# One encoder layer in split float32 on one core: one PSUM tile, accumulators added two banks at a time, wider sums, other ends, and 127 instead of 126 saved-product pairs

## The chip, the cores and the metric

The kernel runs on one core of one Trainium2 chip. The metric is the device time of one execution in microseconds. The engines, with the names that the profile uses, are TensorE (PE; its weight loads are PEld), VectorE (DVE), ScalarE (ACT), GpSimd (POOL) and SyncE (SP, which here only issues transfers). TensorE writes to PSUM, which has eight banks of 512 float32 values per partition.

## The reference

One layer over 256 tokens of width 4096, all in float32. The same normalised input goes through one wide projection, whose columns feed two groups of heads; both outputs are gated and projected back, and a gated embedding is added:

```python
h = rms_norm(x, g_mix)
c_q, c_kv, k_rope, gate_a, q_b, k_b, v_b, gate_b = split(h @ w_in)      # 1024, 512, 64, 5 x 2048
q_a = rms_norm(c_q) @ w_uq ; kv = rms_norm(c_kv) @ w_ukv                # 16 heads, with rotary parts
y_a = rms_norm(softmax attention(q_a, kv)) * silu(gate_a)
y_b = rms_norm(dilated attention(q_b, k_b, v_b), three patterns) * silu(gate_b)
x = x + concat(y_a, y_b) @ w_out                                        # 4096 x 4096
x = x + (p @ w_ple) * sigmoid(rms_norm(x, g_ple) @ w_ple_gate)          # 4096 x 4096
out = rms_norm(x, g_final)
```

## The kernel before

**Products.** To reach float32 accuracy, every operand is kept as two rounded parts, hi and lo. A product of a 128x128 block with a 128x512 block is three matmuls: hi by hi, hi by lo, lo by hi (`mm`). The hi part is a copy on ScalarE, the lo part (the *remainder* below) a subtraction on VectorE (`split`). Weights come from memory in tiles of 128 rows by 1024 columns (512 KB), issued on SP's queue into four slots of `raw_all` and, in some stages, into two lent slots.

**Blocks.** A block (`Block`) is 32 such rows of weights by 1024 columns, multiplied with both halves of the tokens (t = 0, 1) into both halves of the columns (h = 0, 1). A *plain* row (letter `c`) is four products, one for each quarter. Two rows can also be taken as a *pair*: a Strassen-Winograd step that needs seven products instead of eight, at the price of sums of weight blocks (formed on VectorE in the raw slots) and of sums of activation blocks (formed once for a stage by `add_sums`). A pair is four steps, the letters `a`, `b`, `g`, `h`. Each block has an order, a string of these letters. The seven sums M1 to M7 and X take all eight banks: M2, X, M3 and M4 collect the plain rows too. M1, M5, M6 and M7 are mixed into an SBUF tile when the last pair is through (`mix`), and M2, X, M3 and M4 are added to it when the block ends, by four operations, in `d_done`, `gate_done`, `out_done` and `wide_done`. The next block starts with plain rows in the four banks just mixed; its first `a` takes a bank that one of the four adds gives back.

**Stages.** (1) The opening: x is loaded, turned by TensorE and split; small products of zeros run before it (`warm_up`). (2) Six blocks for q, k and v of the dilated heads (ORDER_D). (3) The latents, during which the dilated heads run. (4) Five blocks (ORDER_G): one for the q latent, four for the gates. (5) The latent heads. (6) The output projection (ORDER_O: three blocks, and two chunks of 512 columns without pairs); its result x1 is turned, scaled by g_ple and split, 512 columns at a time (`x1_turn`). (7) Four blocks with w_ple_gate (ORDER_P). Each ends with two rows of w_ple (letter `e`), then the sigmoid by tanh, the addition, and squares for the final norm (`wide_done`). The last one ends in `last_steps`: the rest is done token half by token half, so that the first half can be scaled and stored while the second is multiplied. `finish` forms the reciprocal root of the mean square, `scaled` multiplies and stores.

**Order of the instructions.** Instructions are not issued in the order in which the code makes them. `Metered` notes each with a duration; `Window` holds up to 200 back and lets go the one that can start first by a model of the engines (`Clock`). That the first of a bank's products come before the add which reads it, and the like, is kept by the tile framework: it finds overlapping accesses and sets the waits. Nearly all instructions bear line 293 in the profile, that of the helper which issues them; they are told apart by tiles. Banks are `m`, `s`, `o` and `t`, `lo` and `hi` are weights' parts, `B`, `Ah`, `Al`, `T` and `Q` are slots of SBUF with changing contents.

Of the kernel before, what the change touches and what calls it, by code (L numbers as in the profile page):

```python
# [19 lines left out]
P = 128  # L20
# [18 lines left out]
    "cccccccccccccccccaccccbccabcghghcccc",  # L39
    "ccccaacbbcgchgchcabgabgcahhcbaghcbghcabgacbghhcc",  # L40
    "ccabgcccabgccahbchcagbaghhacbgcbhccaghbabghghccc",
    "ccaaccbbcaghbgcghcccahcbgcaabbghgahbhghccabgchcc",
    "caaccbgabcchcgbchaagbchccbgchcgcahbgacbhaghbghcc",
    "caaccbbcggchhcabgcahbgcaahcbgbachgcbhcabgchgchcc",
# [3 lines left out]
    "ccccccacbacgbhgchabacccgbhghcaacbbgghhcccccc",  # L48
    "cccabccabghccaghbagchccbgcababahgghccbhgcabghhcc",
    "ccacbcccaabgcgchhbcgabgachchbgahbccgcaahbbgghhcc",  # L50
    "cacacbgcbcghahcbacgcbahcbgcgahcbcghahbcgabhcghcc",
)
ORDER_O = (
    "ccccacbgcccabgccacbgccahhcbhgccahabghbcghccc",
    "ccaccbcgcaahcbgcbghcabhcccgahcbaghbagcchbgchcc",
    "caccaccbbccggcabhghhcabcgchabcgacbgcchcahbghcc",
)
ORDER_P = (
    "cccaacccbgbgchhaccbagcahbgcbhgaabcgbhghhaccbghcce",
    "ccabcacbgcghccahbgchacbacgahbgaccbhcgbgahcbhghcce",  # L60
    "cabcccaccgacbghbchgacbahcgchbgabhacgbcghachbghcce",
    "ccabcacgbcghhacbgahbcghacabbcgghhccc",
# [34 lines left out]

class Clock:
# [23 lines left out]
    def ready(self, tag, bufs=1):  # L122
        old = self.tags.get(tag, ())
        return self.last(old[-bufs]) if len(old) >= bufs else 0.0

    @staticmethod
    def place(ap):
        stride = max(1, ap.ap[0][0])
        lo = ap.offset % stride
        return ap.name, lo, lo + 1 + sum((n - 1) * abs(s) for s, n in list(ap.ap)[1:])  # L130

    def after(self, ap, engine, read, alone):
        name, lo, hi = self.place(ap)
        times = [self.base.get(name, 0.0)]
        for m in self.marks.get(name, ()):
            if m[0] < hi and lo < m[1]:
                times += [t for e, t in m[2].items() if e != engine or read or e == "dve"]
                if not alone:
                    times += [t for e, t in m[3].items() if e != engine or e == "dve" and not read]
        return max(times)  # L140

    def mark(self, ap, engine, at, wrote):
        name, lo, hi = self.place(ap)
        marks = self.marks.setdefault(name, [])
        for m in marks:
            if m[0] == lo and m[1] == hi:
                break
        else:
            m = [lo, hi, {}, {}]
            marks.append(m)  # L150
        m[2 if wrote else 3][engine] = at
# [28 lines left out]
class Window:  # L180
# [10 lines left out]
    def push(self, engine, us, outs, ins, late, do, reads):  # L191
        op = Op(self.nr, engine, us, outs, ins, late, do)
        self.nr += 1
        first = set()
        line = engine if engine in self.FIFO else (engine, outs[0].name) if engine == "pe" else None
        if line and not getattr(self.tail.get(line), "gone", True):
            first.add(self.tail[line])
        self.tail[line], op.gone = op, False
        for aps, wrote in ((reads, False), (outs, True)):
            for ap in aps:  # L200
                name, lo, hi = Clock.place(ap)
                both = wrote or ap.space == bass.MemoryType.PSUM
                for other, a, b, w in self.held.get(name, ()):
                    if (both or w) and a < hi and lo < b:
                        first.add(other)
                op.spans.append((name, lo, hi, both))
# [120 lines left out]
def encoder_layer(ctx: ExitStack, tc: tile.TileContext, x, p, positions, g_mix, w_in, g_q_latent, w_uq,  # L327
# [815 lines left out]
    def gate_done(dil, c, blk):  # L1143
        def task():
            e, ps = blk.e, blk.ps
            for t, h, m in QUARTERS:
                nc.vector.tensor_tensor(e[h][:, t], e[h][:, t], ps[m], op=ALU.add)
            yield
            for h in range(2):
                for t in range(NT):  # L1150
                    nc.scalar.activation(e[h][:, t], e[h][:, t], AF.Silu, scale=rx[:, t:t + 1])
                yield
            for h in range(2):
                spawn(gate_rest(dil, c + h, e[h]))
        return task
# [55 lines left out]
    def d_done(key, blk):  # L1211
        def task():
# [3 lines left out]
            for m, t, h in quarters[2:] + quarters[:2] if key == ("v", 1) else quarters:  # L1216
                nc.vector.tensor_tensor(d[h][:, t], blk.ps[m], d[h][:, t], op=ALU.add)
# [48 lines left out]
    def x1_turn(c):  # L1266
# [4 lines left out]
        for b in range(2):  # L1271
# [7 lines left out]
            kts = slice(4 * c + 2 * b, 4 * c + 2 * b + 2)  # L1279
            split_rows(hi[:, 2 * b:2 * b + 2], lo[:, 2 * b:2 * b + 2], tp, G["ple"][:, kts])  # L1280
# [9 lines left out]
    def half_o(c):  # L1290
        def task(ps):
            yield from awaited(("res", c))
            for t in range(NT):
                nc.vector.tensor_tensor(x1[c][:, t], ps[t], x1[c][:, t], op=ALU.add)
            give(*ps.tags)
            yield
        return task

    def done_o(c):
        def task(ps):  # L1300
            for t in range(NT):
                nc.vector.tensor_tensor(x1[c][:, t], ps[t], x1[c][:, t], op=ALU.add)
# [24 lines left out]
    class Block:  # L1327
# [35 lines left out]

        def lend(self):
# [10 lines left out]
        def plain_step(self, kt):  # L1375
# [94 lines left out]
    def add_sums(n, pair, dst, tmp, name, out, free=lambda j: True, first=0):  # L1470
# [3 lines left out]
        def task():  # L1474
# [11 lines left out]
            for j0 in range(first, n, wide):  # L1486
# [3 lines left out]
                work = []  # L1490
                for j in js:
# [4 lines left out]
                for a, u, hi, lo in work:  # L1496
                    two(ALU.add, a, plain(hi), plain(lo))
                for a, u, hi, lo in work:
                    two(ALU.subtract, u[:, 0:3:2], a[:, 1:2].to_broadcast([P, 2, P]), a[:, 0:4:3])
                for a, u, hi, lo in work:  # L1500
                    two(ALU.subtract, u[:, 1], u[:, 2], a[:, 0])
                for a, u, hi, lo in work:
# [58 lines left out]
    def out_done(k, blk):  # L1561
        def task():
            quarters = ((0, 0, "M2"), (1, 1, "X"), (0, 1, "M3"), (1, 0, "M4"))
            for t, h, m in quarters:
                xc = x1[2 * k + h][:, t]
                nc.vector.tensor_tensor(xc, xc, blk.ps[m], op=ALU.add)
# [36 lines left out]
    def x1_sums():  # L1603
        return add_sums(FAST, lambda j: [q[:, 2 * (j % 2):2 * (j % 2) + 2] for q in x1T[j // 2]], z_dst, "B3",
                        "x1_sums", x1_s)
# [58 lines left out]
    def wide_done(k, blk):  # L1664
        def task():
            e, ps = blk.e, blk.ps
            quarters = ((0, 0, 0, "M2"), (3, 1, 1, "X"), (1, 0, 1, "M3"), (2, 1, 0, "M4"))
            for i, t, h, m in quarters:
                nc.vector.tensor_tensor(e[:, i], e[:, i], ps[m], op=ALU.add)
            flags.add(("added", k))  # L1670
            yield
            for n in range(6):
                for i, t, h, m in quarters[n:n + 1]:
                    nc.scalar.activation(e[:, i], e[:, i], AF.Tanh, scale=r1h[:, t:t + 1])
                for i, t, h, m in quarters[n - 1:n] if n else ():
                    u, xc = e[:, i], x1[2 * k + h][:, t]
                    nc.vector.scalar_tensor_tensor(u, u, 1.0, P4[t, h], op0=ALU.add, op1=ALU.mult)
                    nc.vector.tensor_tensor(xc, u, xc, op=ALU.add)
                for i, t, h, m in quarters[n - 2:n - 1] if n > 1 else ():
                    nc.scalar.activation(e[:, i], x1[2 * k + h][:, t], AF.Square, accum_out=ss2[:, t, 2 * k + h:2 * k + h + 1])  # L1680
                if n == 4:
                    flags.add(("wide", k))
                yield
# [230 lines left out]
    x_s, x_s2, z = {}, {}, {}  # L1914

    def xz_dst(j):
        if j > 3:
            return slot(("T0", "T1", "T2", "T3", "T4", "T7")[j - 4], [2, 4, P], F32R)
# [5 lines left out]
    def x_sums():  # L1924
        return add_sums(max(FAST_QKV), x_pair, xz_dst, "B1", "x_sums", x_s,
                        lambda j: ("x", j if j < 4 else 7) in flags and (j < 9 or "rotary" in flags))
# [18 lines left out]
    for n, key in enumerate((key, i) for i in range(2) for key in "qkv"):  # L1945
# [3 lines left out]
                    ("D", (("T5", 1), ("T6", 1)), n == 5), WP + ["B4", "B6", "B0", "B1"] + [("T4", "T7")] * (max(FAST_QKV) < 9))  # L1949
# [4 lines left out]
        if n == 0:  # L1954
            opening = blk
            for x_ in steps[:16]:
                x_.ring = WP
        for at, tag in ((2, "B0"), (3, "B6"), (4, "B4"), (5, "B1")):
            allow(blk, tag, lambda i, at=at, n=n, tag=tag, end=mid_step: (n < at or n == at and i < end) and (
                tag != "B1" or ("x_sums", max(FAST_QKV) - 1) in flags))  # L1960
# [332 lines left out]
```

## Time and profile before

| | |
|---|---|
| three runs | 1886.6, 1886.74 (median), 1888.31 us |
| profiled execution | 1886.92 us |
| its span | 1885.2 us |
| granted clock | 0.998 |
| matmuls | 9103 |
| pairs, by stage | 42 (D), 34 (G), 20 (O), 30 (P): 126 |

The span runs from the first to the last instruction on the core; the execution's own time is 1.7 us longer. Rows of the profile read: engine, line, operation, what is written `<-` what is read, size of a tile as partitions x elements. In the views by time the first two numbers are the start and the length in us. A value in brackets is idle time of the engine before the row and what ended it. In the table by stretches the columns are the stretch, its length, the busy times of PE, PEld, DVE, ACT and POOL with the count of instructions, the granted clock, the DMA share, and GB/s.

### The profile page before, as it was taken

What the parts mean: (1) busy time and instruction counts of PE and PEld (TensorE: products, weight loads), DVE (VectorE), ACT (ScalarE), POOL (GpSimd) and SP (SyncE); (2) the same over time, 40 slices, a digit from 0 to 9 for tenths busy, and PEclk for the clock granted to TensorE, in tenths of its full rate; (3) what the DMA queues carried; (4) which work ended last, traced back from release to release, by engine and by line L of the source; (5) the groups of instructions that cost most, each with busy time, mean ns of one, the idle gap of its engine ahead of it and who ended that gap; (6) DMA issues with size and microseconds to landing.
All of it is one profiled execution on the core that took longest, in us unless ns stands there. A gap on an engine that the chain in (4) does not pass through costs nothing.

```text
span 1885.2 us, 25442 instructions
## 1 busy us (share of the span) xinstructions
PE 1868.0 (99%) x9103; PEld 1575.8 (84%) x9103; DVE 1720.6 (91%) x2333; ACT 1178.7 (63%) x1590; POOL 28.6 (2%) x41
## 2 busy tenths in 40 slices
PE   9999999999999999999999999999999999999996
PEld 7888888888899888888888999888888888888885
DVE  6999999899989989999999777899899989999997
ACT  7666565556688565656566656655556656666664
POOL 0000000000001000000000000000000000000000
PEclk9999999999999999999999999999999999999999
DMA  8666666566735556565667554666666566566674
GB/s 284 217 201 206 217 193 212 190 219 194 216 93 152 177 191 216 182 213 187 213 204 202 137 144 126 197 213 201 213 206 218 181 217 221 190 213 201 200 233 170
DMA packets 160871, 370.58 MB, mean 197 GB/s; under 512 B 29116, under 2 KB 70952, under 8 KB 160744
## 3 DMA queue, kind: packets, MB, share of 16 engines
q1 hardware_dynamic: 159896, 366.58, 61.2%
q0 software_dynamic: 512, 1.84, 0.3%
q8 instruction: 71, 1.16, 0.3%
q10 hardware_dynamic: 336, 0.54, 0.1%
q14 instruction: 56, 0.46, 0.1%
HBM read 364.72 MB, written 4.19 MB: 196 GB/s over the span
## 4 chain that ended last, share of the span: by engine, by line
PE 94%; DVE 3%; DMA 1%; ACT 1%; issue 0%; DVEq 0%; ACTq 0%
PE m L293 54%; PE t L293 19%; PE s L293 12%; PE o L293 10%; DVE lo L293 1%; DMA raw_all<-in_w_ple_dram 1%; DVE T L293 0%; DVE Ah L293 0%; ACT hi L293 0%; DMA raw_all<-in_w_ple_gate_dram 0%; DVE B L293 0%; DMA Al<-in_w_out_dram 0%; DVE Al L293 0%; DVE st L293 0%; DVE raw_all L293 0%
## 5 line engine op out<-in xcount | busy, mean ns | idle before, releaser
L293 ACT ACTIVATE hi<-raw_all 128x1024 fp32r<-128x1024 f32 (+2 forms) x417 | 409.8, 989 | 251.4 <-PE m L293 77.5
L293 DVE TENSOR_TENSOR lo<-raw_all,hi 128x1024 fp32r<-128x1024 f32 (+2 forms) x417 | 468.6, 1133 | 52.7 <-ACT hi L293 49.8
L293 PE MATMUL m<-hi,Ah 128*128 128x512 f32 (+2 forms) x666 | 247.3, 387 | 0.5 <-ACT hi L293 0.5
L293 PE MATMUL m<-hi,Al 128*128 128x512 f32 (+2 forms) x622 | 228.4, 380 | 0.0
L293 PE MATMUL m<-lo,Ah 128*128 128x512 f32 (+2 forms) x543 | 205.4, 378 | 0.9 <-DVE lo L293 0.8
L293 ACT ACTIVATE B<-raw_all 128x1024 fp32r<-128x1024 f32 (+2 forms) x144 | 140.3, 978 | 80.7 <-DVE raw_all L293 23.7
L293 DVE TENSOR_TENSOR raw_all<-raw_all 128x512 f32<-128x512 f32 (+1 forms) x239 | 172.2, 722 | 3.8 <-DMA raw_all<-in_w_out_dram 0.5
L293 DVE TENSOR_TENSOR B<-raw_all,B 128x1024 fp32r<-128x1024 f32 (+2 forms) x144 | 160.8, 1120 | 14.8 <-ACT B L293 14.4
L293 PE MATMUL m<-hi,B 128*128 128x512 f32 (+1 forms) x476 | 164.4, 390 | 0.0
L293 PE MATMUL m<-B,Ah 128*128 128x512 f32 (+2 forms) x560 | 149.1, 359 | 0.0
L293 PEld LDWEIGHTS m<-hi,Ah 128*128 128x128 f32 x666 | 125.3, 188 | 23.4 <-ACT hi L293 1.3
L293 PEld LDWEIGHTS m<-hi,Al 128*128 128x128 f32 x622 | 116.9, 188 | 21.8
L293 PEld LDWEIGHTS m<-lo,Ah 128*128 128x128 f32 x543 | 102.3, 188 | 18.8 <-DVE lo L293 1.6
L293 PEld LDWEIGHTS m<-B,Ah 128*128 128x128 f32 x560 | 97.2, 189 | 14.4
L293 PEld LDWEIGHTS m<-hi,B 128*128 128x128 f32 x476 | 89.2, 188 | 17.7
L293 PE MATMUL m<-B,Al 128*128 128x512 f32 (+2 forms) x286 | 99.2, 371 | 0.0
L293 ACT ACTIVATE hi<-B 128x1024 fp32r<-128x1024 f32 (+1 forms) x65 | 64.6, 999 | 46.3 <-PE m L293 14.0
L293 PE MATMUL m<-lo,B 128*128 128x512 f32 (+1 forms) x238 | 92.2, 387 | 0.0
L293 PE MATMUL t<-hi,Ah 128*128 128x512 f32 x216 | 81.6, 391 | 0.0
L293 DVE TENSOR_TENSOR lo<-B,hi 128x1024 fp32r<-128x1024 f32 (+1 forms) x65 | 74.3, 1145 | 4.7 <-ACT hi L293 3.9
L293 ACT ACTIVATE hi<-T 128x1024 fp32r<-128x1024 f32 (+1 forms) x43 | 44.4, 1038 | 35.1 <-DVE T L293 13.5
L293 PE MATMUL t<-lo,Ah 128*128 128x512 f32 x165 | 64.3, 389 | 0.0
(486 smaller groups left out, 4286.5 us busy)
## 6 DMA issues: line engine op xcount, KB each, us to landing
raw_all<-in_w_in_dram SPq DMA_DIRECT2D x254, 512.0 KB, 4.4
raw_all<-in_w_out_dram SPq DMA_DIRECT2D x98, 512.0 KB, 4.7
raw_all<-in_w_ple_gate_dram SPq DMA_DIRECT2D x90, 512.0 KB, 5.0
T<-in_w_in_dram SPq DMA_DIRECT2D x58, 512.0 KB, 4.5
B<-in_w_in_dram SPq DMA_DIRECT2D x47, 512.0 KB, 4.6
Ah<-in_w_ple_gate_dram SPq DMA_DIRECT2D x38, 512.0 KB, 4.8
raw_all<-in_w_uq_dram SPq DMA_DIRECT2D x48, 256.0 KB, 3.6
B<-in_w_out_dram SPq DMA_DIRECT2D x18, 512.0 KB, 4.8
```

Of the source, the lines that this page charges most:

```text
L293: self.window.push(key, us, outs, ins, late, lambda: do(out, *rest, **named), reads)
```

## The change

1. *PSUM is one tile.* `bank` cuts a bank out of one tile of eight; the order of the banks in it is new, and the planner (`Clock.places`) treats each bank of it by itself. Two banks at any distance can be read by one operation (`banks`, `Block.two`).
2. *Finished accumulators are added two banks at a time*: M2 with M4, then M3 with X, in all four closing functions, and both token halves of a 512-column chunk of the output projection together.
3. *Sums for two pairs at once* in `add_sums`, where a stage asks for it (`x_sums`, `x1_sums`).
4. *x1 remainders:* ScalarE scales the turned columns in place in PSUM, and hi and lo are then formed by one plain copy and one plain subtraction of 512.
5. *`wide_done`* applies tanh to a whole token half at once and joins two of the products with the embedding.
6. *The opening:* the first half of the first two rows of weights is split before the x columns, and the second row is loaded in two halves as the first was.
7. *The end:* for the second token half, `finish` uses Sqrt, a reciprocal and one refinement, instead of an integer estimate and three refinements.
8. *Orders:* most strings are new; the last gate block has nine pairs instead of eight: 127. It also needs a ninth set of sums.

```diff
 ORDER_G = (
...
-    "cacacbgcbcghahcbacgcbahcbgcgahcbcghahcbgcabhcghcc",
+    "cacabaghcbgcbcghhacbagchabcgbhgacbcghhcababgcghhcc",
...
 ORDER_P = (
...
-    "ccabcacgbcghhacbgahbcghacabbcgghhccc",
+    "cccabcgchaabgchbcgahbcghaabcgbghhccc",
...
+BANKS = "m0", "m2", "s", "t0", "m1", "m3", "o", "t1"
...
-    def bank(tag, shape, bufs=1):
-        names[tag] = names.get(tag, 0) + 1
-        return made(lambda: pp.tile([P, *shape], F32, tag=tag, name=f"{tag}_{names[tag]}", bufs=bufs), tag, bufs)
+    psum = pp.tile([P, len(BANKS), 512], F32, tag="psum", name="psum")
+
+    def bank(tag, shape):
+        v = psum[:, BANKS.index(tag), :math.prod(shape)]
...
+    def banks(*tags):
+        a, b = (BANKS.index(t) for t in tags)
+        return psum[:, a:b + 1:b - a]
...
-            for t, h, m in QUARTERS:
-                nc.vector.tensor_tensor(e[h][:, t], e[h][:, t], ps[m], op=ALU.add)
+            for h in range(2):
+                nc.vector.tensor_tensor(e[h], e[h], blk.two(h), op=ALU.add)
...
-            split_rows(hi[:, 2 * b:2 * b + 2], lo[:, 2 * b:2 * b + 2], tp, G["ple"][:, kts])
+            for k in range(2):
+                nc.scalar.activation(tp[:, k], tp[:, k], AF.Copy, scale=G["ple"][:, 4 * c + 2 * b + k:4 * c + 2 * b + k + 1])
+            split(hi[:, 2 * b:2 * b + 2], lo[:, 2 * b:2 * b + 2], tp)
...
+        def two(self, h):
+            return banks(*(self.tags[m] for m in (("M2", "M4"), ("M3", "X"))[h]))
...
-            for lo, n in ((0, Q), (Q, Q)) if self.late and kt == 16 else ((0, 2 * self.q),):
+            for lo, n in ((0, Q), (Q, Q)) if self.late and kt in (16, 17) else ((0, 2 * self.q),):
...
                 if kt in self.front:
-                    self.front.pop(kt)()
                     for h in range(2):
                         split(hi[:, h], lo[:, h], box[0][:, h])
+                        if h == 0:
+                            self.front.pop(kt)()
...
+                if twice:
+                    a, u = both[:, :, :4], both[:, :, 4:]
+                    hi, lo = (q.rearrange("p (j k) (t c) -> p j (k t) c", j=2, t=NT) for q in both_at(j0))
+                    two(ALU.add, a, plain(hi), plain(lo))
+                    two(ALU.subtract, u[:, :, 0:3:2], a[:, :, 1:2].to_broadcast([P, 2, 2, P]), a[:, :, 0:4:3])
...
+            nc.scalar.activation(e[:, 2:], e[:, 2:], AF.Tanh, scale=r1h[:, 1:])
+            yield
+            nc.scalar.activation(e[:, :2], e[:, :2], AF.Tanh, scale=r1h[:, :1])
+            nc.vector.scalar_tensor_tensor(e[:, 2:], e[:, 2:], 1.0, banks("t0", "t1"), op0=ALU.add, op1=ALU.mult)
...
     def finish(t, a):
         r, h, w = r2[:, t:t + 1], stat(1), stat(1)
-        bits = r.bitcast(I32)
-        nc.vector.tensor_scalar(bits, a.bitcast(I32), -0.5, float(0x5F3759DF), op0=ALU.mult, op1=ALU.add)
         nc.vector.tensor_scalar(h, a, -0.5, None, op0=ALU.mult)
-        for _ in range(3):
+        if t:
+            nc.scalar.activation(w, a, AF.Sqrt)
+            nc.vector.reciprocal(r, w)
+        else:
+            nc.vector.tensor_scalar(r.bitcast(I32), a.bitcast(I32), -0.5, float(0x5F3759DF), op0=ALU.mult, op1=ALU.add)
+        for _ in range(1 if t else 3):
             nc.vector.scalar_tensor_tensor(w, r, r, h, op0=ALU.mult, op1=ALU.mult)
             nc.vector.scalar_tensor_tensor(r, w, 1.5, r, op0=ALU.add, op1=ALU.mult)
```

More of the change, by code (lines that the diff above doesn't have):

```diff
@@ L126, in place, with places @@
     @staticmethod
[L127 to L130, printed above, removed]
-    def after(self, ap, engine, read, alone):
[L133 to L139, printed above, removed]
+    def places(ap):
+        dims = list(ap.ap)
+        lo, name = ap.offset % max(1, dims[0][0]), ap.name
+        if name[:4] != "psum":
+            return [(name, lo, lo + 1 + sum((n - 1) * abs(s) for s, n in dims[1:]))]
+        n, dims = (dims[1], dims[2:]) if len(dims) > 2 and dims[1][0] >= 512 else ((0, 1), dims[1:])
+        width = 1 + sum((n - 1) * abs(s) for s, n in dims)
+        starts = [lo + k * n[0] for k in range(n[1])]
+        return [(f"psum{a // 512}", a % 512, a % 512 + width) for a in starts]
@@ L140, in after @@
+    def after(self, ap, engine, read, alone):
+        times = [0.0]
+        for name, lo, hi in self.places(ap):
+            times.append(self.base.get(name, 0.0))
+            for m in self.marks.get(name, ()):
+                if m[0] < hi and lo < m[1]:
+                    times += [t for e, t in m[2].items() if e != engine or read or e == "dve"]
+                    if not alone:
+                        times += [t for e, t in m[3].items() if e != engine or e == "dve" and not read]
         return max(times)
@@ L142, in mark @@
     def mark(self, ap, engine, at, wrote):
[L143 to L151, printed above, removed]
+        for name, lo, hi in self.places(ap):
+            marks = self.marks.setdefault(name, [])
+            if wrote and name[:4] == "psum":
+                marks[:] = [m for m in marks if m[0] < lo or hi < m[1]]
+            for m in marks:
+                if m[0] == lo and m[1] == hi:
+                    break
+            else:
+                m = [lo, hi, {}, {}]
+                marks.append(m)
+            m[2 if wrote else 3][engine] = at
@@ L200, in push @@
             for ap in aps:
-                name, lo, hi = Clock.place(ap)
                 both = wrote or ap.space == bass.MemoryType.PSUM
[L203 to L206, printed above, removed]
+                for name, lo, hi in Clock.places(ap):
+                    for other, a, b, w in self.held.get(name, ()):
+                        if (both or w) and a < hi and lo < b:
+                            first.add(other)
+                    op.spans.append((name, lo, hi, both))
         for name, *span in op.spans:
@@ L1215, in task @@
             quarters = ("M2", 0, 0), ("X", 1, 1), ("M3", 0, 1), ("M4", 1, 0)
[L1216 to L1217 removed]
+            for h in range(2):
+                nc.vector.tensor_tensor(d[h], blk.two(h), d[h], op=ALU.add)
             yield from awaited("rx")
@@ L1292, in task @@
             yield from awaited(("res", c))
-            for t in range(NT):
-                nc.vector.tensor_tensor(x1[c][:, t], ps[t], x1[c][:, t], op=ALU.add)
+            nc.vector.tensor_tensor(x1[c], banks(*ps.tags), x1[c], op=ALU.add)
             give(*ps.tags)
@@ L1300, in task @@
         def task(ps):
-            for t in range(NT):
-                nc.vector.tensor_tensor(x1[c][:, t], ps[t], x1[c][:, t], op=ALU.add)
+            nc.vector.tensor_tensor(x1[c], banks(*ps.tags), x1[c], op=ALU.add)
             give(*ps.tags)
@@ L1563, in task @@
             quarters = ((0, 0, "M2"), (1, 1, "X"), (0, 1, "M3"), (1, 0, "M4"))
-            for t, h, m in quarters:
-                xc = x1[2 * k + h][:, t]
-                nc.vector.tensor_tensor(xc, xc, blk.ps[m], op=ALU.add)
+            for h in range(2):
+                xc = x1[2 * k + h]
+                nc.vector.tensor_tensor(xc, xc, blk.two(h), op=ALU.add)
             yield
```

113 lines of the change are left out of this document (68 added, 45 removed).

## The prediction

> **What bounds the kernel now.** I read the page first, then the table by stretches, the waits of TensorE, the chain of waits, and last the instructions in order of time at both ends and at one boundary of two blocks.
>
> ```profile
> span 1885.2 us, 25442 instructions
> PE 1868.0 (99%) x9103; PEld 1575.8 (84%) x9103; DVE 1720.6 (91%) x2333; ACT 1178.7 (63%) x1590; POOL 28.6 (2%) x41
> PE m L293 <- DVE junk L293: 1.5, 1, 1.5
> PE m L293 <- DVE lo L293: 1.0, 2, 0.8
> PE m L293 <- ACT hi L293: 0.5, 1, 0.5
> PE s L293 <- ACT T L293: 0.4, 1, 0.4
> 236.93 6.12 PE m L293 x27
> ```
>
> The first two rows are the page's; the next four are all that TensorE waited for (total, times, longest); the last is a stretch of the chain. TensorE is busy 99% of the span, and its waits that have a name come to 3.4 us. In the chain 27 products of 512 columns take 6.12 us, 0.227 each. So time comes off in three ways only: fewer matmuls, fewer of those few waits, and a shorter head and tail where TensorE does not yet, or no longer, run. Shorter work on VectorE or ScalarE is worth nothing by itself.
>
> The profiled execution took 1886.92 us, 1.7 more than its span. That is 0.18 above the median of the runs (1886.74), so I add the terms to 1886.92 and take 0.2 off at the end.
>
> **The extra pair.** The orders hold 126 pairs before (42+34+20+30) and 127 after; the new one is the ninth of the last gate block. Two plain rows of weights cost eight products, a pair seven; each product is three matmuls. Three matmuls of 0.227 are **0.68 us less**, the only matmuls that go. The price is on VectorE:
>
> ```profile
> 936.45 0.68 DVE L293 TENSOR_TENSOR B7b<-B7b,o 128x512 f32<-128x512 f32 x1
> 937.05 0.68 DVE L293 TENSOR_TENSOR B7b<-B7b,t 128x512 f32<-128x512 f32 x1
> 938.85 1.22 DVE L293 TENSOR_TENSOR lo<-raw_all,hi 128x1024 fp32r<-128x1024 f32 x1
> 939.98 1.22 DVE L293 TENSOR_TENSOR B<-raw_all,B 128x1024 fp32r<-128x1024 f32 x1
> 1572.00:1654.00 82.00, 82.00 (x364) 67.89 (x363) 79.69 (x94) 52.16 (x64) 0.00 (x0) 1.00 0.62 207
> 934.00:1016.00 82.00, 82.00 (x364) 67.89 (x363) 76.54 (x89) 49.38 (x53) 0.00 (x0) 1.00 0.66 194
> ```
>
> Starts of adjoining operations lie 0.60 apart for 512 elements and 1.13 for 1024. A pair has one remainder of 512, three of 1024 and four sums of 512: 0.60 + 3.39 + 2.40 = 6.4. Two plain rows have two remainders, 2.26. So VectorE gets about 4.1 us more in this block. The last row is that block: VectorE (the third busy time) works 76.5 of 82 us and rests 5.5. After: 5.5 - 4.1 - 0.7 of shorter block + 0.1 saved by the merged adds leaves 0.8. The row above it is a block of the last stage, where 2.3 us of rest were enough for TensorE to lose nothing; 0.8 is beyond anything this trace shows. I put 0.2 us of new waiting there; between 0 and the 1.5 that are missing against 2.3. The ninth pair's own sums (four operations of up to 512 and one remainder, about 3 us) fall to earlier blocks with 5 us of rest.
>
> **Merged adds, one PSUM tile.** A block ends with four adds of an accumulator; now two adds take two banks each. From the rows above that is 1.13 instead of 1.20 us, 0.07 each, some 38 times: 2.7 us of VectorE under a running TensorE, worth nothing. What it adds is a wait. The first add takes M2 and M4, and M4 is the block's last product:
>
> ```profile
> 934.31 0.39 PE L293 MATMUL t<-hi,Al 128*128 128x512 f32 x1
> 935.25 0.68 DVE L293 TENSOR_TENSOR B7a<-B7a,s 128x512 f32<-128x512 f32 x1
> 937.25 0.62 PE L293 MATMUL s<-B,Ah 128*128 128x512 f32 x2
> ```
>
> Here the block before ends at 934.70, the add of M2 (bank s) starts 0.55 later anyway, and bank s is written again at 937.25, when the next block opens its first pair. With two banks the add ends near 936.5 and still leaves 0.7. Behind a waiting add on VectorE stand the remainders of the next block's first rows, and TensorE waits for those. I take 0; the bounds are 0 and the third rival's price.
>
> **Two-pair sums, x1 remainders.**
>
> ```profile
> L293 ACT ACTIVATE T<-t 128x512 fp32r<-128x512 f32 x56 | 33.3, 595 | 12.4 <-PE t L293 11.9
> L293 DVE SCALAR_TENSOR_TENSOR Al<-t,gT,Ah 128x256 fp32r<-128x256 f32 x30 | 13.1, 476 | 1.0 <-ACT Ah L293 0.9
> ```
>
> The remainder of two x1 columns is now one plain subtraction of 512 instead of two scaled ones of 256 at 0.48, so VectorE saves 0.2; ScalarE scales in place and then copies, 0.6 more (first row). Sixteen times that is 3 us less on VectorE and 10 us more on ScalarE, which rests 37% of the span. Each chunk is ready some 0.4 us later; the rows of weights that need it come microseconds later. The wide closing of the last stage and the sums of two pairs cut VectorE's fixed part by under 0.1 per operation. Together 0; if ScalarE had no rest where they fall, each of the 16 would cost up to 0.6, and nothing in the trace points to that.
>
> **The head.**
>
> ```profile
> 5.28 1.31 PE L293 MATMUL m<-junk 128*128 128x512 bf16 x3
> 6.21 0.62 PE L293 MATMUL m<-hi,Ah 128*128 128x512 f32 x1
> 6.93 0.50 PE L293 MATMUL m<-lo,Ah 128*128 128x512 f32 x1
> 7.28 0.40 PE L293 MATMUL m<-hi,Al 128*128 128x512 f32 x1
> 4.48 0.20 ACT L293 ACTIVATE gT<-t 128x32 f32<-128x32 f32 x1 [1.97 <-PE t L293]
> 5.16 0.47 ACT L293 ACTIVATE Ah<-s,gT 128x256 fp32r<-128x256 f32 x1 [0.49 <-PE s L293]
> 6.19 1.29 DVE L293 TENSOR_TENSOR lo<-raw_all,hi 128x512 fp32r<-128x512 f32 x2
> ```
>
> From the first to the third product pass 1.07 us where two steps of 0.227 would be 0.46: 0.61 is lost, because the weights' first remainder runs at 6.19, behind the scaled copy of x. After, the first half of the weights goes ahead: its copy fits into ScalarE's pause after 4.68, its remainder starts near 5.4 and is done by 6.1. The three warm-up products still hold TensorE until 6.2, so nothing before that is won. **0.5 us**, between 0 and 0.6. The second row of weights also comes in halves: one more issue on SP's queue, ahead of loads that are needed later.
>
> **The tail.**
>
> ```profile
> 1872.31 0.49 ACT L293 ACTIVATE Ah<-Ah,st 128x256 f32<-128x256 f32 x1
> 1876.05 1.33 ACT L293 ACTIVATE T<-T,st 128x512 f32<-128x512 f32 x2 [3.25 <-DVE st L293]
> 1874.21 0.46 DVE L293 TENSOR_SCALAR st<-st 128x1 f32<-128x1 f32 x3
> 1874.71 1.31 DVE L293 SCALAR_TENSOR_TENSOR st<-st 128x1 f32<-128x1 f32 x6
> 1057.96 0.17 DVE L293 RECIPROCAL st<-st 128x2 f32<-128x2 f32 x1 [2.60 <-ACT T L293]
> ```
>
> The reciprocal root of the last 128 tokens takes from 1874.21 to 1876.05, and all that is left to scale and store waits for it. After: the mean (0.25), a Sqrt on ScalarE (0.20, as the small copy at 4.48), a reciprocal (0.20), one refinement instead of three (a third of 1.35, 0.45), two hand-overs of some 0.05: 1.2 instead of 1.85. **0.65 us less**, at most 0.75, if the function table of Sqrt is loaded in ScalarE's 3.25 us of rest. Loads of tables in this trace:
>
> ```profile
> 98.21 1.28 ACT L293 ACT_TABLE_LOAD   x1
> 99.77 0.26 ACT L293 ACTIVATE ss<-T 128x64 f32<-128x64 f32 x1 [0.28 <-DVE T L293]
> 1055.43 1.28 ACT L293 ACT_TABLE_LOAD   x1 [2.13 <-DVE st L293]
> 1056.73 0.56 ACT L293 ACTIVATE T<-s,st 128x256 f32<-128x256 f32 x1
> ```
>
> At 98.21 the load ran at once, and only the activation behind it waited for VectorE. At 1055.43 the load itself stood 2.13 us behind VectorE. There the activation reads PSUM too; the new Sqrt reads one value of VectorE alone, like the first, so I take the first: loaded from 1872.8 to 1874.1, before 1874.46. [...]
>
> **The new orders, above all in the last block.**
>
> ```profile
> 1848.17 0.86 PE L293 MATMUL s<-Ah,B 128*128 128x512 f32 x3
> 1849.54 0.49 PE L293 MATMUL m<-hi,Ah 128*128 128x512 f32 x1 [0.50 <-ACT hi L293]
> 1850.79 0.50 PE L293 MATMUL m<-lo,Ah 128*128 128x512 f32 x1 [0.77 <-DVE lo L293]
> 1824.64 0.39 PE L293 MATMUL m<-hi,Al 128*128 128x512 f32 x1
> 1825.25 0.50 PE L293 MATMUL m<-lo,Al 128*128 128x512 f32 x1 [0.22 <-DVE lo L293]
> 1841.25 7.07 DMA raw_all<-in_w_ple_dram
> ```
>
> Against steps of 0.227, TensorE loses 0.69 before 1849.54, 1.02 before 1850.79 and 0.38 before 1825.25, with some 0.2 of restart: 2.3 us. The last row (the chain) shows why: a load of w_ple issued at 1841.25 landed 7.07 us later. The loads are issued when VectorE has read a slot, so a late VectorE makes late loads. The new order begins this block with three plain rows instead of two, keeps the two lent slots two steps longer, and the merged work spares VectorE 0.2 us. I take **1.0 us less**. The bounds are all 2.3 back and as much again.
>
> **The sum.** -0.68 + 0.2 - 0.5 - 0.65 - 1.0 = -2.6; 1886.92 - 2.6 = 1884.3, against the median 1884.1.
>
> **Rivals.** (1) The orders remove the last block's waits wholly: -0.68 - 0.6 - 0.75 - 2.3 = -4.3, 1882.4. For it: the waits are few and at one place. Against: they come from a queue of loads whose number does not change. (2) Sqrt's table load stands behind VectorE's signal as at 1055.43: 1.28 more, 1885.4. Against: the row at 98.21. [...] (3) The slow one: a merged add gives the bank back too late. Five blocks open their pair after one plain row (2.72 us). The row at 935.25 left 0.7 of slack; with one remainder (1.13) more before the add TensorE waits 0.4, with two 1.5. Five times 1.5 is 7.7: 1891.8. It decides from two on; one gives 1886.2. Against: the planner that orders the instructions knows this bank, and the slack shown. (4) The waits treat the one PSUM tile as a span, so that TensorE stands from 934.53 until both adds are over, near 937.6: 3.1 us at 17 block ends, 53 us, 1937. Nothing before shows such a view. (5) The last block gets as much worse: 1884.1 + 1.0 + 2.3 = 1887.4, with the new saturated gate block on top at most 1888.7.
>
> **How the numbers follow.** Forecast 0.38, rivals 0.25, 0.17, 0.07, 0.03 and 0.10. A measurement of this kernel tells about 0.2% from no change, 3.8 us: faster lies below 1883.0, slower above 1890.5. Faster holds most of (1), 0.21, and the low edge of the forecast, 0.07: 0.28. Slower holds (3) and (4): 0.10. The rest, 0.62, is no change. The range 1881.7 to 1887.6 takes in (1), (2) and most of (5).
>
> **What would show it.** 9100 products on TensorE instead of 9103; the third product 0.46 us after the first; the load of Sqrt's table right behind the last tanh and the root 1.2 us after its mean; VectorE over 97% in the last gate block, with TensorE's waits there; TensorE's waits after 1820. I am wrong if TensorE waits at block ends for an accumulator's add, or if all named waits exceed 5 us.

## The result, and the profile after

| | before | after |
|---|---|---|
| median of the runs | 1887.45 us (4 runs) | 1937.17 us (4 runs, 1934.37 to 1939.61) |
| ratio | | 1.0263, 95% interval 1.0247 to 1.0273 |
| profiled span | 1885.2 us | 1937.8 us |
| matmuls | 9103 | 9100 |
| VectorE operations | 2333 | 2259 |

The kernel became 2.6% slower. The forecast was 1884.1 us; the number that came true is the fourth rival's, 1937, to which I had given a chance of 0.03. That its sum fits so closely is partly luck, as the waits below show.

The page of the kernel after, its span and the busy times:

```profile
span 1937.8 us, 25374 instructions
PE 1884.3 (97%) x9100; PEld 1577.0 (81%) x9100; DVE 1727.9 (89%) x2259; ACT 1194.0 (62%) x1604; POOL 30.2 (2%) x41
```

VectorE has 74 operations fewer, yet its busy time did not fall: a wide operation costs nearly what its two halves cost (1.13 us against 1.20 in the prediction's rows), and the ninth pair's sums came on top. TensorE's share fell from 99% to 97%: it stands still now. What it waits for is told by the waits of TensorE after (total, times, longest):

```profile
PE psum L306 <- DVE B L306: 21.7, 20, 2.9
PE psum L306 <- DVE T L306: 8.8, 9, 1.4
PE psum L306 <- DVE B7a L306: 3.6, 3, 1.3
PE psum L306 <- DVE B7b L306: 2.9, 3, 1.3
PE psum L306 <- DVE junk L306: 1.5, 1, 1.5
```

The first four rows, which the kernel before did not have, come to 37.0 us; all its named waits were 3.4 us. `B`, `T`, `B7a` and `B7b` are the tiles to which finished accumulators are added. They are 35 waits of at most 2.9 us, about 1 us each, and not 17 of 3.1 as the fourth rival has it: its place and its sum came true, its price only at the first block end. The rest of the 50 us goes with the restart behind each wait (after the one at 188.28 the next product starts 0.34 us later instead of 0.227) and with stretches at half the clock (0.50 near 106 us, 0.51 near 191, 0.57 near 794); how it divides was not measured. The instructions in order of time, TensorE and VectorE, where the first block ends:

```profile
101.95 0.39 PE L306 MATMUL psum<-B,Al 128*128 128x512 f32 x1
102.74 2.35 DVE L306 TENSOR_TENSOR B<-psum,B 128x1024 f32<-128x1024 f32 x2
105.24 0.76 PE L306 MATMUL psum<-hi,Ah 128*128 128x512 f32 x1 [2.90 <-DVE B L306]
105.80 0.63 PE L306 MATMUL psum<-lo,Ah 128*128 128x512 f32 x1
...
107.93 0.57 PE L306 MATMUL psum<-hi,Ah 128*128 128x512 f32 x1
108.34 0.40 PE L306 MATMUL psum<-lo,Ah 128*128 128x512 f32 x1
```

The block's last product starts at 101.95. The next block's weights are ready, and its first product goes to a bank that neither merged add reads, yet it starts at 105.24, behind both adds (102.74 to 105.09). From start to start that is 3.29 instead of 0.227: 3.06 us lost; the prediction's price for rival 4 was 3.1. The products behind it are 0.43 apart instead of 0.227, up to 108.34. The table by stretches says why; the eighth column is the granted clock:

```profile
102.00:105.00 3.00, 0.34 (x2) 0.00 (x0) 3.00 (x3) 1.69 (x3) 0.00 (x0) 0.98 0.83 253
106.50:108.00 1.50, 1.50 (x5) 1.11 (x5) 1.50 (x3) 1.50 (x3) 0.00 (x0) 0.50 0.09 38
108.00:110.00 2.00, 2.00 (x10) 1.62 (x9) 2.00 (x4) 0.82 (x2) 0.00 (x0) 0.93 0.75 193
190.00:197.00 7.00, 5.95 (x14) 4.70 (x15) 5.69 (x6) 1.91 (x3) 0.00 (x0) 0.51 0.53 174
```

Behind the stall TensorE is granted half the clock (0.50), and once more after the second block's end (0.51).

Both ends did what was predicted. The instructions after, the opening and then the last reciprocal root:

```profile
6.05 0.58 PE L306 MATMUL psum<-hi,Ah 128*128 128x512 f32 x1
6.46 0.39 PE L306 MATMUL psum<-lo,Ah 128*128 128x512 f32 x1
6.69 0.40 PE L306 MATMUL psum<-hi,Al 128*128 128x512 f32 x1
...
1925.67 0.49 ACT L306 ACTIVATE Ah<-Ah,st 128x256 f32<-128x256 f32 x1
1926.18 1.28 ACT L306 ACT_TABLE_LOAD   x1
1927.58 0.40 DVE L306 TENSOR_SCALAR st<-st 128x1 f32<-128x1 f32 x2
1927.82 0.20 ACT L306 ACTIVATE st<-st 128x1 f32<-128x1 f32 x1 [0.36 <-DVE st L306]
1928.70 1.33 ACT L306 ACTIVATE T<-T,st 128x512 f32<-128x512 f32 x2 [0.68 <-DVE st L306]
```

The third product starts 0.64 after the first (1.07 before, 0.46 at best) and the first 0.16 earlier: 0.59 gained. From the start of the mean to the scaling pass 1.12 us instead of 1.84. From the last matmul to the end of the span it is 12.83 us instead of 13.58.

### The profile page after: what moved, and what is told of

It is laid out like the page before. It is cut to its first block, busy times and chain, and to the rows that moved or that the text cites. A ratio compares the mean times of both kernels' runs of the same rounds, so it can differ in the third digit from the quotient of the medians.

```text
span 1937.8 us, 25374 instructions
## 1 busy us (share of the span) xinstructions
PE 1884.3 (97%) x9100; PEld 1577.0 (81%) x9100; DVE 1727.9 (89%) x2259; ACT 1194.0 (62%) x1604; POOL 30.2 (2%) x41
## 3 DMA queue, kind: packets, MB, share of 16 engines
q0 software_dynamic: 512, 1.84, 0.3%
## 4 chain that ended last, share of the span: by engine, by line
PE 85%; DVE 10%; issue 2%; ACT 1%; DMA 1%; DVEq 0%; ACTq 0%; SPq 0%
PE psum L306 85%; DVE B L306 3%; DVE lo L306 2%; DVE T L306 2%; DVE raw_all L306 1%; ACT hi L306 1%; DMA raw_all<-in_w_in_dram 0%; DVE Ah L306 0%; DVE B7b L306 0%; DVE Al L306 0%; DMA raw_all<-in_w_ple_dram 0%; ACT T L306 0%; DVE st L306 0%; DMA raw_all<-in_w_out_dram 0%; ACT B L306 0%
## 5 line engine op out<-in xcount | busy, mean ns | idle before, releaser
L306 PE MATMUL psum<-hi,Ah 128*128 128x512 f32 (+2 forms) x1089 | 403.9, 392 | 18.4 <-DVE B L306 9.5
L306 PE MATMUL psum<-hi,Al 128*128 128x512 f32 (+2 forms) x965 | 355.3, 385 | 2.6 <-DVE B7a L306 1.3
L306 PE MATMUL psum<-lo,Ah 128*128 128x512 f32 (+2 forms) x875 | 337.4, 386 | 6.1 <-DVE B L306 2.6
L306 PEld LDWEIGHTS psum<-hi,Ah 128*128 128x128 f32 x1089 | 205.7, 189 | 65.7 <-DVE T L306 9.8
L306 PE MATMUL psum<-hi,B 128*128 128x512 f32 (+1 forms) x754 | 254.4, 390 | 1.3 <-DVE B L306 0.7
L306 PE MATMUL psum<-B,Ah 128*128 128x512 f32 (+2 forms) x847 | 237.9, 370 | 2.3 <-DVE B7b L306 1.3
L306 PEld LDWEIGHTS psum<-hi,Al 128*128 128x128 f32 x965 | 182.6, 189 | 39.2 <-DVE B7a L306 1.7
L306 PEld LDWEIGHTS psum<-lo,Ah 128*128 128x128 f32 x875 | 165.9, 190 | 38.4 <-DVE B L306 3.4
L306 PEld LDWEIGHTS psum<-B,Ah 128*128 128x128 f32 x847 | 151.1, 189 | 28.6 <-DVE B7b L306 1.8
L306 PE MATMUL psum<-B,Al 128*128 128x512 f32 (+2 forms) x482 | 167.0, 379 | 2.6 <-DVE B7a L306 1.3
```

The costliest lines, as they stand in the source:

```text
L306: self.window.push(key, us, outs, ins, late, lambda: do(out, *rest, **named), reads)
```

## The experiments

Two questions were open: which part of the change makes TensorE stand, and whether the rest brings the 2.6 us that I forecast. Each run's time stands beside a median of the kernel before on the same chip (1886.91 to 1887.73).

**1. Without the two-bank operations.** The other closing functions and the second tanh gate go back in the same way.

```diff
-            for h in range(2):
-                nc.vector.tensor_tensor(e[h], e[h], blk.two(h), op=ALU.add)
+            for t, h, m in QUARTERS:
+                nc.vector.tensor_tensor(e[h][:, t], e[h][:, t], ps[m], op=ALU.add)
...
```

> The changed kernel with every two-bank operation on VectorE undone: the accumulators are added one bank at a time again, in the order of before, and the second tanh gate is multiplied bank by bank; the one PSUM tile, the new orders, both ends and the x1 sums stay. Theory W (an operation over two banks of the one tile is held apart from products into every bank of that tile): without such operations there is nothing to be held apart; TensorE's waits on VectorE's adds at block ends go from about 37 us back to a few, and the time is my forecast, about 1884.5 us (1882 to 1888). Theory S (held apart only from products into banks between its two) and theory A (the two-bank operation itself gives its banks back too late) say the same here. Theory O (one tile for all banks costs by itself, also for single-bank operations) says about 1937 us. Theory N (the loss comes from the new orders, the head or the tail) says about 1937 us too.

Measured 1893.32 us, ratio 1.0033 (1.0022 to 1.0045). 44 of the 50 us are the two-bank operations. One tile for all of PSUM is not what costs (theory O falls). But 1893 is not 1884.5: some 6 us more than before come from elsewhere, against 2.6 less that I had forecast.

**2. Neighbouring banks.** The banks get new numbers, and X and M4 change their places; two lines left out here let the planner cut a contiguous access into its banks. Every operation stays.

```diff
-BANKS = "m0", "m2", "s", "t0", "m1", "m3", "o", "t1"
+BANKS = "m0", "m1", "m2", "m3", "s", "o", "t0", "t1"
...
-        NAMES = "M2", "X", "M3", "M4", "M1", "M5", "M6", "M7"
+        NAMES = "M2", "M4", "M3", "X", "M1", "M5", "M6", "M7"
```

> The changed kernel with the banks numbered so that the two banks of every merged operation are neighbours: no bank lies between them any more; one PSUM tile and the merged operations stay. Theory S: no product is held up by a merged operation on other banks, about 1884.5 us (1882 to 1888), TensorE's named waits on VectorE's adds a few us. Theory W: every merged operation still holds up the products into the six other banks: about 1937 us (1925 to 1945), 25 to 40 us of named waits. Theories A, O and N: about 1937 us.

Measured 1894.24 us, ratio 1.0033 (1.002 to 1.0047): the same as without the operations. The same block end in this kernel, in order of time:

```profile
102.68 0.39 PE L308 MATMUL psum<-hi,Ah 128*128 128x512 f32 x1
102.85 2.35 DVE L308 TENSOR_TENSOR B<-psum,B 128x1024 f32<-128x1024 f32 x2
102.91 0.39 PE L308 MATMUL psum<-lo,Ah 128*128 128x512 f32 x1
...
105.17 0.39 PE L308 MATMUL psum<-hi,Al 128*128 128x512 f32 x1
```

The adds take the same 2.35 us, and TensorE multiplies under them without a gap. W falls, and S holds: a merged add holds up products into its two banks and *all banks between them*. After the change M2 and M4 of the first block are banks 0 and 5 of the tile, M3 and X banks 1 and 4, and the next block's plain rows go to 2, 6, 3 and 7. So half of the banks that TensorE wants next lie inside; at the end of the second block it is 4 and 5 between 2 and 7.

One more reading would fit these times: that an add of two banks apart counts as one of all eight. The kernel after decides against it. At the end of its fourth block the adds take banks 2 and 7, and 3 and 6; the next block opens with bank 0, outside both, and goes on with bank 4, inside both:

```profile
356.70 1.22 DVE L306 TENSOR_TENSOR B<-psum,B 128x1024 f32<-128x1024 f32 x1
356.98 0.39 PE L306 MATMUL psum<-hi,Ah 128*128 128x512 f32 x1
357.21 0.39 PE L306 MATMUL psum<-lo,Ah 128*128 128x512 f32 x1
357.44 0.39 PE L306 MATMUL psum<-hi,Al 128*128 128x512 f32 x1
357.97 0.50 PE L306 MATMUL psum<-hi,Ah 128*128 128x512 f32 x1
```

The three matmuls for bank 0 run under the first of the adds (356.70 to 357.92); the first one for bank 4 starts when it is over.

**3. Four tiles of two banks.**

```diff
-    psum = pp.tile([P, len(BANKS), 512], F32, tag="psum", name="psum")
+    psum = [pp.tile([P, 2, 512], F32, tag="psum" + q, name="psum" + q) for q in "ABCD"]
```

> The same as the kernel with neighbouring banks, but PSUM is four tiles of two banks instead of one tile of eight, so that a merged operation's tile holds only the two banks that it adds. Theories W and S: a merged operation holds up only products into its own two banks; about 1884.5 us (1881 to 1888), named waits on VectorE's adds a few us. Theory A (the merged operation itself is what costs, since a bank comes free 0.5 us later): about 1937 us. Theory O: between the two at most. Theory N: about 1937 us.

> The kernel with four PSUM tiles of two banks, without any two-bank operation. Theory T (in a tile that is smaller than all of PSUM, a read of one bank holds up products into the tile's other bank): the waits in the heads' stages stay, about 1940 to 1945. Theory M (the merged operations cost there after all): about 1893.

Measured 1944.69 us, ratio 1.0302 (1.0284 to 1.0319), and without any two-bank operation 1951.58 us, ratio 1.034 (1.0326 to 1.0354). W and S missed by 60 us. A and N come near the size, but the waits are not where they put them: most lie in the heads' stages, and taking out the merged operations, in the second run, makes nothing faster. T, which was formed on the first trace, holds. The instructions of the first of these kernels in the latent heads' stage, and then the two largest waits of TensorE in the second:

```profile
1071.52 0.40 PE L310 MATMUL psumA<-B,hi 128*128 128x256 f32 x2
1072.02 0.69 DVE L310 TENSOR_TENSOR B<-psumA,B 128x512 fp32r<-128x512 f32 x1 [1.11 <-PE psumA L310]
1072.77 0.38 PE L310 MATMUL psumA<-B,lo 128*128 128x256 f32 x1 [0.85 <-DVE B L310]
```

```profile
PE psumC L310 <- DVE T L310: 4.9, 6, 1.0
PE psumD L310 <- DVE T L310: 4.2, 8, 0.9
```

The matmul at 1072.77 is the third of a product whose first two have run, and it waits for VectorE's reading of the same tile. The program reads a bank only when its product is finished, so VectorE reads the other one. An operation that reads *one* bank of a two-bank tile holds up the products into the tile's other bank, here by 0.85 us. In the heads' stages, where the two banks of a tile serve different units, this happens over and over. So the tile of all eight banks tells its banks apart when an operation stays in one of them (1893.32 us without two-bank operations), while the smaller tiles do not (1951.58 us, also without).

**4. The merges alone, apart and neighbouring.** To the kernel before are added only the one tile and the two-bank adds; the second run numbers the banks as in experiment 2. Orders, wide steps, x1 remainders and both ends stay as before.

```diff
+    psum = pp.tile([P, len(BANKS), 512], F32, tag="psum", name="psum")
...
-            for t, h, m in QUARTERS:
-                nc.vector.tensor_tensor(e[h][:, t], e[h][:, t], ps[m], op=ALU.add)
+            for h in range(2):
+                nc.vector.tensor_tensor(e[h], e[h], blk.two(h), op=ALU.add)
...
```

> The kernel of before with one part of the change alone: PSUM as one tile and the accumulators of closed blocks and units added two banks at a time (38 two-bank operations); the orders of before with 126 pairs, the wide steps of before behind the adds, and both ends of before. Theories W, S and A: the whole loss is in this part, about 1935 us (1925 to 1945) against 1887.5, with 25 to 40 us of TensorE's named waits on VectorE's adds and stretches of products at half the granted clock behind the longest of them. Theory O: about the same. Theory N: about 1887.5 us (1886 to 1890), no new waits.

> The kernel of before with one PSUM tile and the two-bank adds, as in the run of the merges alone, but with the banks numbered so that the two of each merged add are neighbours. Theory S (a merged add holds up products into all banks between its two): the 50 us of the run of the merges alone vanish; 1887.5 to 1889, TensorE's named waits 3 to 6 us. If the neighbours are not what counts: 1935 or more.

Measured 1938.74 us, ratio 1.0279 (1.0261 to 1.0296), against 1889.59, ratio 1.0011 (1.0002 to 1.0019). The merges with banks apart cost 51 us against the median beside them, and the numbering of the banks alone is worth 49 of these. And the merged adds are not free even side by side: 2 to 3 us. Two waits of TensorE that the kernel before does not have show where some of it is lost, in the output projection; in the second, TensorE turns x1 and waits until the add of both token halves is through:

```profile
1495.18 0.50 PE L308 MATMUL psum<-lo,B 128*128 128x512 f32 x1 [0.66 <-DVE lo L308]
...
1524.81 0.65 PE L308 MATMUL psum<-ident,T 128*128 128x128 f32 x4 [0.60 <-DVE T L308]
```

**5. The x1 remainders.** Undone in the kernel of experiment 2, and made alone in the kernel before.

```diff
-            for k in range(2):
-                nc.scalar.activation(tp[:, k], tp[:, k], AF.Copy, scale=G["ple"][:, 4 * c + 2 * b + k:4 * c + 2 * b + k + 1])
-            split(hi[:, 2 * b:2 * b + 2], lo[:, 2 * b:2 * b + 2], tp)
+            kts = slice(4 * c + 2 * b, 4 * c + 2 * b + 2)
+            split_rows(hi[:, 2 * b:2 * b + 2], lo[:, 2 * b:2 * b + 2], tp, G["ple"][:, kts])
```

> The kernel with neighbouring banks, with the x1 remainders of before (scaled copy and scaled subtraction of 256 columns each, nothing scaled in place). Theory X (the bank in which x1 is turned comes back later by the in-place scaling, and TensorE's next product wants that bank): the two waits of TensorE at 1322 and 1414 us of that kernel (2.2 and 2.6 us, and half-clock products behind the second) go; some 5.5 to 6.5 us less, 1887 to 1888. Theory R (the new orders of the output projection put the product behind the turn, whatever the remainder costs): the waits stay, 1893.

> The kernel of before with the x1 remainders of the change alone. Theory X: waits of TensorE for a turned bank appear in the output projection here too, some 2 to 6 us more, 1890 to 1893. Theory R: no such waits, 1887.3. My prediction's step: 0.

Measured 1890.96 us, ratio 1.0016 (1.0007 to 1.0025), and 1890.13, ratio 1.0012 (1.0003 to 1.002). Undoing gains 3 us, making it alone costs 2 to 3: theory X. It is not the whole of it, though: X put the first run at 1887 to 1888, and of the two waits named, the one at 1322 went, the one at 1414 stayed. The kernel of experiment 2 at that place, in order of time:

```profile
1413.98 0.40 PE L308 MATMUL psum<-hi,B 128*128 128x512 f32 x1
1414.24 0.91 ACT L308 ACTIVATE psum<-psum,gT 128x256 f32<-128x256 f32 x2
1415.18 0.60 ACT L308 ACTIVATE B<-psum 128x512 fp32r<-128x512 f32 x1
1416.21 0.69 DVE L308 TENSOR_TENSOR B<-psum,B 128x512 fp32r<-128x512 f32 x1
1416.95 0.80 PE L308 MATMUL psum<-hi,B 128*128 128x512 f32 x1 [2.57 <-DVE B L308]
```

x1 is turned in a bank that a block uses too. TensorE's next product goes into this bank and waits for the scaling (0.91), the copy (0.60), a stretch in which VectorE finishes another remainder, and the subtraction (0.69). With the old remainders it waits just as long, since VectorE is behind by three other operations:

```profile
1412.91 0.87 DVE L308 SCALAR_TENSOR_TENSOR B<-psum,gT,B 128x256 fp32r<-128x256 f32 x2
1413.84 0.50 PE L308 MATMUL psum<-hi,B 128*128 128x512 f32 x1 [2.71 <-DVE B L308]
```

Alone in the kernel before, the change of the remainders makes a new wait at another turn (1320 us). In the waits of TensorE it is the row

```profile
PE o L293 <- DVE Al L293: 1.7, 1, 1.7
```

**6. The orders of the output projection.** The kernel of experiment 5's first run, with the three strings of ORDER_O of before.

```diff
-    "ccccacbccabgcgccacbgccahhbhgcccabghhabcghccc",
-    "ccacbccgcahcbaghcbgcabhcacgcbghchabagcchbgchcc",
-    "caccaccbbcggccabhghhcabcgcabcchgabgcahchbgchcc",
+    "ccccacbgcccabgccacbgccahhcbhgccahabghbcghccc",
+    "ccaccbcgcaahcbgcbghcabhcccgahcbaghbagcchbgchcc",
+    "caccaccbbccggcabhghhcabcgchabcgacbgcchcahbghcc",
```

> The kernel with neighbouring banks and the x1 remainders of before, with the three orders of the output projection of before as well. Theory R for the wait at 1411 us (2.7 us, which stayed when the x1 remainders were undone): the new orders put a product into the bank of the turn right behind it; it goes, and 1890.96 becomes 1887 (1886 to 1888). Otherwise it stays and the time is 1891.

Measured 1888.09 us, ratio 1.0006 (0.9997 to 1.0015), just above the range expected. The wait of 2.71 is gone; the span falls from 1889.4 to 1886.2, with one wait of 0.8 more at 1494. So this wait, which began at 1411, belonged to the new orders.

**7. The parts with a gain, alone.** The kernel before with the last stage's orders and both ends of the change; the first run also has the ninth pair (the first string below) and its ninth set of sums. `finish` and the opening are as the change has them.

```diff
-    "cacacbgcbcghahcbacgcbahcbgcgahcbcghahbcgabhcghcc",
+    "cacabaghcbgcbcghhacbagchabcgbhgacbcghhcababgcghhcc",
...
-    "cccaacccbgbgchhaccbagcahbgcbhgaabcgbhghhaccbghcce",
-    "ccabcacbgcghccahbgchacbacgahbgaccbhcgbgahcbhghcce",
-    "cabcccaccgacbghbchgacbahcgchbgabhacgbcghachbghcce",
-    "ccabcacgbcghhacbgahbcghacabbcgghhccc",
+    "cccaccacbgbgchahcbcagbcahgcbhgabcgabhchgcahbgchce",
+    "ccabcacbcgcghchabcgachbacgahbgaccbhgcbgahcbhghcce",
+    "cabcaccccgbgachhbcgacbhacbgagcbhghahcbcgahcbghcce",
+    "cccabcgchaabgchbcgahbcghaabcgbghhccc",
...
+            nc.scalar.activation(w, a, AF.Sqrt)
+            nc.vector.reciprocal(r, w)
```

> The kernel of before with only those parts of the change that I gave a gain: the ninth pair of the last gate block, the orders of the four blocks with w_ple_gate, the split of the first weights ahead of x, and the end with Sqrt; PSUM, adds, sums and x1 remainders of before. My prediction's terms: -0.68 (pair), +0.2 (VectorE's last gate block), -0.5 (head), -0.65 (tail), -1.0 (waits of the last block): 1887.3 - 2.6 = 1884.7, between 1883 and 1886. If the terms don't add up or the orders need the merged adds: 1887 or more.

> The kernel with the gaining parts alone, without the ninth pair and its ninth set of sums (126 pairs, all orders but the last stage's as before). Theory P (the ninth pair costs more on VectorE than its three matmuls save: a wait of 1.2 us at 786 us, where the ninth sums are formed, and 0.5 in the last gate block): no wait at 786, 1.0 us less than with it: 1885.3 (1884 to 1886). My prediction's terms (pair -0.68 +0.2): 0.5 us more than with it: 1887.0.

Measured 1886.52 us with the pair, ratio 0.9993 (0.9984 to 1.0002), half a microsecond above the range expected, and **1885.02 us without it, ratio 0.9988 (0.9979 to 0.9997)**: the second is the one version that is faster than the kernel before beyond its interval, and so faster than both. It is 1.9 us, 0.1%. The two spans are 1884.5 and 1883.3. The two ratios' intervals overlap, so what the pair does is read from the traces. VectorE's and TensorE's rows with the pair, some 16 us behind the ninth sums:

```profile
787.39 0.68 DVE L293 TENSOR_TENSOR B<-B,t 128x512 f32<-128x512 f32 x1
788.13 0.50 PE L293 MATMUL t<-hi,T 128*128 128x512 f32 x1 [1.01 <-DVE B L293]
```

At 764 to 771 VectorE forms the ninth set (four sums and a remainder, as predicted). After that the last turn of a gate runs at 785.82 instead of 782.60, and the multiplication with the turned gate, which frees bank `t`, at 787.39 instead of 784.52. Without the pair TensorE has no wait there, and up to this place the two kernels differ in the ninth set alone. The last gate block reads, with the pair and without:

```profile
935.00:1017.00 82.00, 81.75 (x362) 67.24 (x361) 80.31 (x93) 50.67 (x56) 0.00 (x0) 1.00 0.64 194
```

```profile
933.90:1015.90 82.00, 82.00 (x365) 67.99 (x364) 76.57 (x89) 49.60 (x54) 0.00 (x0) 1.00 0.64 192
```

VectorE works 3.74 us more (predicted 4.1), and TensorE waits for a remainder once, at 951.65. The pair saves 0.68 us of matmuls and costs 1.2 and 0.5 us of waiting and restart at these two places: a loss of about 1.

**8. All the merged and wide work, with the banks side by side.** The kernel of experiment 6 with ORDER_D and ORDER_G of before too, so with 126 pairs.

```diff
-    "ccacbccgcaabcgchhbcgahbgachcbghcacbcaagbbghghhcc",
-    "cacabaghcbgcbcghhacbagchabcgbhgacbcghhcababgcghhcc",
+    "ccacbcccaabgcgchhbcgabgachchbgahbccgcaahbbgghhcc",
+    "cacacbgcbcghahcbacgcbahcbgcgahcbcghahbcgabhcghcc",
...
```

> The changed kernel with neighbouring banks, x1 remainders of before, and all orders of before except those of the last stage (126 pairs): it keeps the merged adds, the sums of two pairs, the wide closing of the last stage, both ends. If the merged and widened VectorE work is worth nothing, as I predicted, the time of the kernel with the gaining parts alone: 1885.3 (1884 to 1887). If shorter VectorE work helps the places where TensorE waits for it: up to 1 us less.

Measured 1888.17 us, ratio 1.0004 (0.9996 to 1.0013), against 0.9988 for the same gaining parts without merged operations: the one tile, the merged adds, the sums of two pairs and the wide closing together cost some 3 us, where 1885.3 was expected. The sizes of this and experiment 4's second run agree.

## Why the prediction was wrong

**The step that failed** is "Merged adds, one PSUM tile", and in it the sentence "What it adds is a wait". I asked only whether the two banks that an add reads come back in time, and took 0, between 0 and the third rival. I did write down the fourth rival, with its place (17 block ends), its price (3.1 us) and its sum (1937), and then dismissed it because "Nothing before shows such a view". Nothing before could show it: no operation before touches two banks. A missing row is no evidence against a new wait. The diff had what was needed: it set the two banks of nearly every add apart in one tile (0 and 5, 1 and 4 in the first block), and the front of this document says that the waits are set by the tile framework, not by the planner, which had been taught to treat each bank by itself. The runs showed in place of the step: +51 us by the merges alone, +2 to 3 with neighbouring banks.

**What the change came to**; behind the first row, ratios of the runs times 1887 us:

| step | from | us |
|---|---|---|
| banks apart instead of neighbours | 1937.17 - 1894.24 | +43 |
| x1 remainders | 1.0033 to 1.0016 | +3 |
| orders of the output projection | 1.0016 to 1.0006 | +2 |
| other orders with the ninth pair | 1.0006 to 1.0004 | under 1 |
| one tile, merged adds, wide sums and closing | 1.0004 to 0.9988 | +3 |
| last stage's orders and both ends | 0.9988 to 1 | -2 |

The single steps below the first are about as small as the uncertainty of such a difference (each ratio has some 1.7 us either way); that they are there rests on the waits in the traces.

**The other terms.**
- *The pair*, -0.68 + 0.2: the matmuls went (9100), the last gate block lost 0.5 rather than 0.2, and "the ninth pair's own sums ... fall to earlier blocks with 5 us of rest" was wrong: 1.2 us came back as a wait. A block's rest is not there at the moment when the sums are due.
- *x1 remainders*, 0, "up to 0.6" each: the price was put on ScalarE's busy time. It fell on a bank: the turned columns sit in PSUM until the last reader is through, and the product that wants this bank waits up to 2.2 us at one turn.
- *The head*, -0.5: 0.59 measured, 0.16 of it from an earlier first product, where the prediction had said that nothing could be won. *The tail*, -0.65, at most 0.75: 0.75 measured.
- *The last block's waits*, -1.0: in experiment 7's second kernel TensorE loses 1.5 us beyond steps of 0.227 after 1800 us, where it lost 2.7 before: 1.2 gained. The two waits that remain there:

```profile
1848.57 0.73 PE L293 MATMUL m<-hi,Ah 128*128 128x512 f32 x2 [0.44 <-ACT hi L293]
1849.83 0.50 PE L293 MATMUL m<-lo,Ah 128*128 128x512 f32 x1 [0.53 <-DVE lo L293]
```

- *Other orders*, not costed by themselves: the output projection's lost some 2 us.

So three of the four gaining terms were right in sign and about in size, and the pair was wrong in sign. Without the pair they come to 0.5 + 0.65 + 1.0 = 2.15 by the prediction, and the kernel with them alone is 1.9 us faster than the median beside it. With the pair, which the forecast counted as 0.48 gained, it is 1.2 us.

**The rivals.** The first and the fifth fell where the merges are not in the way: of the last block's waits some are left, and they did not grow. The second (the load of Sqrt's table behind VectorE's signal) fell: in the rows above the load starts 0.02 us after the activation before it ends, at 1926.18, and is done at 1927.46; Sqrt waits 0.36 more, for VectorE's mean alone. The third (a bank given back too late) did not show at the merged adds, but a bank given back too late is what the x1 turn and the ninth sums cost. The fourth had the mechanism of most of the 50 us; the span is not the whole tile, but reaches from the first bank of an add to its last.

**What I said would show it.** The products (9100) and the root's 1.2 us (1.12) came as said; the third product came 0.64 us after the first, not 0.46. VectorE's share of the last gate block is 98% in the first kernel of experiment 7 (80.31 of 82 us), with a wait of TensorE there, as said too. The other sign came too: "I am wrong if TensorE waits at block ends for an accumulator's add, or if all named waits exceed 5 us": there were such waits, and all named waits are 40.5.

## What to carry to other kernels

Where an operation is made to span several banks or buffers of one tile, ask what the tool that sets the waits counts as touched: everything between may count (here 1937.17 us with the banks apart, 1894.24 side by side), so put what is read together side by side, and check the first boundary in the trace. A planner that knows better than the tool that sets the waits did not help here: it treated each bank by itself, and TensorE still waited 37.0 us. And an engine's rest over a block did not pay for extra work (VectorE rested 5.8 of 81.8 us where the ninth sums went, and they still cost 1.2): look for who holds the bank or slot that the bottleneck wants at that very moment.

## What the hardware showed that I had not expected

A stall of TensorE cost more than its length here. After 2.90 us without a product (102.34 to 105.24) the next ones came 0.43 apart at a granted clock of 0.50 until 108.34, about 1.5 us more. Behind two waits of 1.32 us, at 188.28 and 191.05, the clock was 0.51 too. The length alone does not decide: in experiment 2 a wait of 2.57 us was followed by half the clock, in experiment 5 one of 2.71 us in the same place by products 0.23 apart. The two stretches, half clock first:

```profile
1417.00:1419.00 2.00, 2.00 (x5) 1.63 (x6) 0.00 (x0) 0.36 (x1) 0.00 (x0) 0.50 0.75 248
```

```profile
1413.00:1415.00 2.00, 1.16 (x5) 0.99 (x6) 0.78 (x2) 0.16 (x1) 0.00 (x0) 1.00 0.66 209
```

What decides it stays open here.
